# A static scheduler's numbers, the order of the DeltaNet weights and projections issued in passes

## The chip, the cores and the metric

The kernel runs on one core of one Trainium2 chip. The metric is the device time of one execution in microseconds (us), the median of the runs shown. TensorE is the matrix engine (PE in the profile), VectorE is DVE, ScalarE is ACT, GpSimd is POOL, and SyncE (SP) issues most of the transfers.

## What is computed

One sequence of 512 tokens with 1024 channels goes through three layers:

- a layer with dilated band attention and attention to a memory of 256 tokens, then a gated feed-forward network of width 2816;
- a layer whose mixer is a gated DeltaNet with six heads of width 128, in both directions, with the same kind of memory attention, then another feed-forward network;
- a last mixer with gated linear attention, a state-space part and sparse attention, whose sum is projected and added.

The DeltaNet is what matters here, cut to its core:

```python
qkv, z, gate_in, q_mem = split(h @ w_in)
q, k, v = silu(conv5(qkv))                  # q and k also normalized per head
a   = I + strict_lower((k*beta) k^T * decay)   # per head, direction and chunk of 64
sol = triangular_solve(a, [v*beta, k*beta*exp(g)])
for chunk in chunks:                        # the state is carried from chunk to chunk
    v_new = u - w @ state
    out   = (q*exp(g)) @ state + intra @ v_new
    state = state*exp(g_last) + (k*exp(g_last-g))^T @ v_new
o = rmsnorm(o_fwd + o_bwd) * out_norm * silu(z)
```

## The kernel before, in words

All matrices are float32. A projection keeps the precision by splitting each operand into a high and a low part: `wh` is the weight rounded by ScalarE (L243), `wl` is the rest, subtracted by VectorE (L262), and likewise `Xh` and `Xl` for the activations. `mm3` (L268) then issues three matmuls in a row into one bank of PSUM, low weight by high activation (L271), high by low (L272) and high by high (L273). A projection of one weight of 1024 by 128 is eight such blocks of 512 columns. A weight comes as one transfer of 512 KB (L207), through three raw buffers and four split ones.

**The order of the work** is made by `Flow` (L56). Every piece of work is a Python generator that yields requests: an engine and a planned duration, a buffer or bank from a set (`get`, `two`), or an event (`wait`). `Flow.run` keeps a planned free time for each engine. It takes the request that could start first, and among those of the same engine within `DELTA` of it the one with the lowest `late` number; the generator then writes its instructions. So the order of the instructions on each engine is fixed when the program is written, and the chip runs each engine's list in order, waiting where an operand is not there. `HOP` (L63) is the planned time between two engines, and L96 adds 0.07 us where an operation of an engine other than TensorE follows one of its own. `act`, `dve` and `pool` (L151 to L160) are planned durations by elements.

**DeltaNet** (L1168) begins with `projector` (L1775), the generator that projects the weights in the order that `deltanet_weights` (L1158) gives, with `late` 20, so that it fills TensorE where nothing else is ready. The first four weights are done in two halves of tokens. Each result holds one of two banks (`mm`) until it is taken. For each head:

- `key` convolves the projection (four vector operations, L1322), normalizes it and makes the transposed key `kTh`, the scaled copies `ktd` and the products of keys `kk`. Two heads may hold `kTh` and `ktd`; they are given back when a head's chains end.
- `decays` makes for each direction the decay `AT` and the strict lower part `Ln`. It takes a `px` bank for each direction in turn, of three.
- `query` makes `qTh` and the product `kq`, and holds a `px` bank until the decays of both directions are there. `value` and `gate` make `vtok` and `zt` (two heads).
- `inverse` (L1483) inverts the 64-row triangles in six levels and one merging step. A level is 16 small products and four transposes (L1508, L1512), two copies by ScalarE (L1519), 16 products (L1533) and two predicated copies by VectorE (L1537). Each half takes two of three `lv` banks. Two threads run it, one for the even heads and one for the odd ones (`inv=2`). Its result goes to `Uf`, of which there is one.
- `chain` (L1569), one for each direction, carries the state through four chunks (L1580, L1583, L1588, L1591, L1595) and holds a `px` bank all the time. `gate_out` normalizes, transposes and multiplies by the gate (L1645).

`memory` is the attention to the memory (L841), and `splits` prepares the output projection (L1691, L1693). The last mixer uses `projector` too, for 15 single weights and some pieces of two.

Of the kernel before, what the change touches and what calls it, by code (L numbers as in the profile page):

```python
# [35 lines left out]
S = 512  # L36
D = 1024
KT = D // P
# [13 lines left out]

DELTA = 0.1


class Flow:  # L56
# [5 lines left out]

    HOP = 0.2  # L63

# [28 lines left out]
    def start(self, eng, toks):  # L93
        s = self.free[eng]
        for at, e in toks:
            s = max(s, at + (self.HOP if e != eng else 0.0 if e == "PE" else 0.07))  # L96
        return s

    def run(self):
        while self.threads:  # L100
# [39 lines left out]
            s, t = min(ops, key=lambda x: x[0])  # L140
            s, t = min((x for x in ops if x[1]["req"][0] == t["req"][0] and x[0] <= s + DELTA), key=lambda x: x[1]["late"])
            eng, cost = t["req"][:2]
            self.free[eng] = s + cost
            t["tok"] = (s + cost, eng)
# [18 lines left out]
class K:  # L163
# [132 lines left out]
    def inputs(self, F, W, eX, eM, eF, pro):  # L296
# [93 lines left out]
        def memory():  # L390
            yield "late", 0.5
            for l in range(2):
                yield "wait", *eN[l]
                for c in range(2):
                    ev = W["mk"][l][c]
                    yield "wait", ev
                    yield "get", "mm"
                    p = self.psum("mm")
                    w = ev["W"]
                    for k in range(KT):  # L400
                        t = yield "PE", 0.33
                        self.mm3(p[:, :256], (w.h[:, k, :], w.l[:, k, :]), (M[l].h[:, k, :], M[l].l[:, k, :]),
                                 k == 0, k == KT - 1)
                    F.put("wsl", t)
                    F.add(evac(self.memK[l][:, c, :], p), 0.5, t)
                yield "wait", *W["mv"][l]
                for u in range(2):
                    yield "get", "mm"
                    p = self.psum("mm")
                    ts = slice(u * P, (u + 1) * P)  # L410
                    for k in range(KT):
                        w, kk = W["mv"][l][k // 4]["W"], k % 4
                        t = yield "PE", 0.33
                        self.mm3(p[:, :256], (M[l].h[:, k, ts], M[l].l[:, k, ts]), (w.h[:, kk, :], w.l[:, kk, :]),
                                 k == 0, k == KT - 1)
                    F.add(evac(self.memV[l][:, u, :], p, l == 1 and u == 1), 0.5, t)
                for _ in range(2):
                    F.put("wsl", t)
# [118 lines left out]
    def attention(self, F, W, eX, eM, eB, at, e2):  # L537
# [41 lines left out]
        def group(g):  # L579
# [37 lines left out]
            for i, t0 in enumerate((0, 64, 192, 320, 384)):  # L617
                yield "get", "mm"
                p = self.psum("mm")
                for k in range(KT):  # L620
                    w, kk = W2[k // 4]["W"], k % 4
                    t = yield "PE", 0.33
                    self.mm3(p[:, :256], (X.h[:, k, t0:t0 + P], X.l[:, k, t0:t0 + P]), (w.h[:, kk, :], w.l[:, kk, :]),
                             k == 0, k == KT - 1)
                F.add(copy_v(g, i, p[:, :256], r["t"][2][:, i, :], "mm"), g - 0.5, t)
# [394 lines left out]
    def out_ffn(self, F, i, W, gnext, groups, kev, before):  # L1020
# [57 lines left out]
        for part, (f0, f1) in enumerate(self.PARTS):  # L1078
# [22 lines left out]
            while f < nf:  # L1101
                fs = (f, f + 1) if part == 0 and f == 0 else (f,)
                banks = {}
                for hv in ((0, 256), (256, 512)) if len(fs) == 2 else ((0, 512),):
# [3 lines left out]
                    for f_ in fs:  # L1108
                        for z in range(2):
# [6 lines left out]
                            for k in range(KT):  # L1116
                                tk = yield "PE", 0.65 * (t1 - t0) / 512
                                self.mm3(p[:, t0:t1], (ev["W"].h[:, k, :], ev["W"].l[:, k, :]),
                                         (X.h[:, k, t0:t1], X.l[:, k, t0:t1]), k == 0, k == KT - 1)
# [38 lines left out]
    def deltanet_weights(self):  # L1158
# [4 lines left out]
        r["m"] = [self.weight(w, 0, KT, 3096 + c * P, P) for c in range(2)]  # L1163
        N = 3
        heads = [[r[n][h] for n in ("kqvz" if h < N else "kqv")] for h in range(6)]
        return r, [r["g"]] + sum(heads[:3], []) + r["m"] + sum(heads[3:], []) + r["z"][N:]

# [589 lines left out]
    def proj(self, F, ev, eX, m=P):  # L1757
# [7 lines left out]
        for t0, t1 in rngs:  # L1765
            yield "wait", *eX[t0 // P:t1 // P]
            for k in range(KT):
                t = yield "PE", 0.65 * (t1 - t0) / S
                self.mm3(p[:m, t0:t1], (W.h[:, k, :], W.l[:, k, :]), (X.h[:, k, t0:t1], X.l[:, k, t0:t1]),
                         k == 0, k == KT - 1)  # L1770
# [4 lines left out]
    def projector(self, F, items, eX, eP, late=20, haste=0):  # L1775
# [5 lines left out]

        X = self.X
        yield "late", late

        def part(it, t0, t1):
            W, m = it["W"], it["args"][4]
            yield "wait", *eX[t0 // P:t1 // P]
            for k in range(KT):
                t = yield "PE", 0.65 * (t1 - t0) / S
                self.mm3(it["p"][:m, t0:t1], (W.h[:, k, :], W.l[:, k, :]), (X.h[:, k, t0:t1], X.l[:, k, t0:t1]),  # L1790
                         k == 0, k == KT - 1)
            if t1 == S:
# [13 lines left out]
        for i, it in enumerate(items):  # L1806
# [13 lines left out]
            for u in range(4):  # L1820
# [4 lines left out]
                for k in range(KT):  # L1825
                    W, kk = it[k // 4]["W"], k % 4
                    t = yield "PE", 0.33
                    self.mm3(p[:, :256], (X.h[:, k, sl], X.l[:, k, sl]), (W.h[:, kk, :], W.l[:, kk, :]),
# [394 lines left out]
    def s5(self, F, W, eX, open_, eY, uT):  # L2223
# [140 lines left out]
        def glu():  # L2364
# [14 lines left out]
            for c in range(2):  # L2379
                zs = []  # L2380
                for o in (2, 0):
# [3 lines left out]
                    for k in range(2):  # L2385
                        t = yield "PE", 0.65
                        self.mm3(p, (w.h[:, k, os_], w.l[:, k, os_]), yh[k], k == 0, k == 1)
# [898 lines left out]
```

## Time and profile before

| | us |
|---|---|
| median of 3 runs (1770.24 to 1770.43) | 1770.36 |
| the profiled execution | 1771.96 |
| its span from the first to the last instruction | 1770.2 |
| TensorE busy | 1718.8 |
| VectorE busy | 951.0 |
| ScalarE busy | 797.4 |
| GpSimd busy | 276.0 |

In the profile a busy time is a union: the end of a matmul is modelled, and the next one begins before it, so a row of matmuls is read by the time from start to start. "PEclk" is the granted share of TensorE's clock, 1.00 for 2.4 GHz and 0.50 for 1.2 GHz, as a mean over the stretch. An idle time is put down to the instruction that ended it.

### The profile page before, as it was taken

To read this page: it belongs to the slowest core of one execution; us is meant where nothing else is said; L and a number is where in the kernel's file an instruction comes from. 1 tells how busy PE (TensorE), PEld (TensorE's weight loads), DVE (VectorE), ACT (ScalarE), POOL (GpSimd) and SP (SyncE) were. 2 spreads that over 40 slices of the span, in tenths; PEclk is the share of its full clock that TensorE was granted. 3 is DMA by queue.
4 is the path that set the end of the run, shared out by engine and by line. 5 is a ranking of instruction groups with operands and counts; after the bars stand their busy time and mean duration, and the time that the engine had idled before them with its cause. 6 is when DMAs were issued, how large, how long until landed. Compare 5 with 4: busy or idle time off the path is not lost.

```text
span 1770.2 us, 30809 instructions
## 1 busy us (share of the span) xinstructions
PE 1718.8 (97%) x12391; PEld 1431.1 (81%) x12391; DVE 951.0 (54%) x1895; ACT 797.4 (45%) x1922; POOL 276.0 (16%) x440
## 2 busy tenths in 40 slices
PE   6999999999999999999999899999999999999999
PEld 5988679888888887787877778888888888888787
DVE  6333656323333378756765467464433468467573
ACT  5443635333222247657666455333222353345671
POOL 5200001000000020000000152375540033210000
PEclk8999999999999999999999999999999999999999
DMA  6513133333233333102010165344333253552012
GB/s 194 152 51 96 49 119 96 119 96 95 96 95 96 96 119 84 50 26 61 26 49 26 33 157 141 104 146 134 106 108 102 80 154 112 151 160 70 25 37 84
DMA packets 211983, 167.88 MB, mean 95 GB/s; under 512 B 21996, under 2 KB 183036, under 8 KB 211840
## 3 DMA queue, kind: packets, MB, share of 16 engines
q1 hardware_dynamic: 203808, 154.39, 29.6%
q0 software_dynamic: 4560, 9.42, 2.1%
q10 hardware_dynamic: 3472, 2.10, 0.4%
q8 instruction: 97, 1.59, 0.4%
q14 instruction: 46, 0.38, 0.1%
HBM read 152.23 MB, written 13.65 MB: 94 GB/s over the span
## 4 chain that ended last, share of the span: by engine, by line
PE 89%; DVE 6%; ACT 2%; issue 2%; DMA 1%; POOL 1%; ACTq 0%; SPq 0%; DVEq 0%; POOLq 0%
PE bk L271 23%; PE bk L272 23%; PE bk L273 23%; PE x L1508 1%; PE x L1512 1%; PE y L1533 1%; PE no L2740 1%; PE npT L2723 1%; DVE wl L262 1%; DVE hs L940 1%; PE chain L1588 1%; PE ns L2709 1%; PE hT L947 1%; PE ns L2707 1%; PE o L1608 1%
## 5 line engine op out<-in xcount | busy, mean ns | idle before, releaser
L262 DVE TENSOR_TENSOR wl<-raw,wh 128x512 fp32r<-128x512 f32 x450 | 314.7, 740 | 386.7 <-ACT wh L243 386.3
L243 ACT ACTIVATE wh<-raw 128x512 fp32r<-128x512 f32 x474 | 273.0, 622 | 532.9 <-PE bk L273 296.6
L271 PE MATMUL bk<-Xh,wl 128*128 128x512 f32 (+2 forms) x1312 | 494.6, 377 | 0.2 <-ACT Xh L949 0.2
L272 PE MATMUL bk<-Xl,wh 128*128 128x512 f32 (+2 forms) x1312 | 477.9, 364 | 0.5 <-DVE Xl L954 0.3
L273 PE MATMUL bk<-Xh,wh 128*128 128x512 f32 (+2 forms) x1312 | 478.0, 364 | 0.0
L271 PEld LDWEIGHTS bk<-Xh,wl 128*128 128x128 f32 (+1 forms) x1312 | 247.0, 188 | 40.1 <-issue 4.1
L273 PEld LDWEIGHTS bk<-Xh,wh 128*128 128x128 f32 (+1 forms) x1312 | 246.7, 188 | 39.8
L272 PEld LDWEIGHTS bk<-Xl,wh 128*128 128x128 f32 (+1 forms) x1312 | 247.3, 188 | 34.6 <-DVE Xl L954 0.9
L271 PE MATMUL bk<-wh,Xl 128*128 128x512 f32 (+1 forms) x424 | 152.6, 360 | 7.9 <-DVE Xl L794 3.7
L272 PE MATMUL bk<-wl,Xh 128*128 128x512 f32 (+1 forms) x424 | 145.4, 343 | 0.4 <-DVE wl L262 0.4
L273 PE MATMUL bk<-wh,Xh 128*128 128x512 f32 (+1 forms) x424 | 145.5, 343 | 0.0
L271 PE MATMUL bk<-wh,Al 128*128 128x512 f32 x352 | 139.7, 397 | 0.0
L272 PE MATMUL bk<-wl,Ah 128*128 128x512 f32 x352 | 139.5, 396 | 0.0
L273 PE MATMUL bk<-wh,Ah 128*128 128x512 f32 x352 | 138.6, 394 | 0.0
L919 POOL TENSOR_TENSOR nc<-ncm,nhalf 128x1 f32<-128x1 f32 x16 | 11.6, 726 | 666.8 <-DVE ncm L917 664.4
L271 PEld LDWEIGHTS bk<-wh,Xl 128*128 128x128 f32 x424 | 84.9, 200 | 19.2 <-DVE Xl L794 3.1
L1091 DVE TENSOR_TENSOR sg<-sg,bk 128x512 f32<-128x512 f32 x44 | 30.2, 688 | 124.4 <-PE bk L273 119.9
L272 PEld LDWEIGHTS bk<-wl,Xh 128*128 128x128 f32 x424 | 85.0, 201 | 7.7 <-DVE wl L262 1.1
L273 PEld LDWEIGHTS bk<-wh,Xh 128*128 128x128 f32 x424 | 84.6, 200 | 8.0
L271 PEld LDWEIGHTS bk<-wh,Al 128*128 128x128 f32 x352 | 66.0, 188 | 16.1
L273 PEld LDWEIGHTS bk<-wh,Ah 128*128 128x128 f32 x352 | 66.0, 188 | 16.1
L272 PEld LDWEIGHTS bk<-wl,Ah 128*128 128x128 f32 x352 | 66.1, 188 | 15.3
(577 smaller groups left out, 2590.9 us busy)
## 6 DMA issues: line engine op xcount, KB each, us to landing
raw<-in_ffn_w_gate_up_dram SPq DMA_DIRECT2D x88, 512.0 KB, 3.8
raw<-in_ffn_w_down_dram SPq DMA_DIRECT2D x44, 512.0 KB, 3.4
raw<-in_dn_w_in_dram SPq DMA_DIRECT2D x27, 512.0 KB, 3.8
raw<-in_att_w_in_dram SPq DMA_DIRECT2D x20, 512.0 KB, 3.9
raw<-in_w_in_dram SPq DMA_DIRECT2D x20, 512.0 KB, 3.7
raw<-in_mem_w_kv_dram SPq DMA_DIRECT2D x8, 512.0 KB, 3.5
raw<-in_att_w_out_dram SPq DMA_DIRECT2D x8, 512.0 KB, 3.3
xd<-x SPq DMA_DIRECT2D x8, 512.0 KB, 2.6
```

The lines of the kernel that those rows point to most:

```text
L243: nc.scalar.activation(wh[:, sl], ev["raw"][:, sl], AF.Copy)
L262: eng.tensor_tensor(wl[:, sl], raw[:, sl], wh[:, sl].bitcast(F32), op=OP.subtract)
L271: mm(out, A[1], B[0], start=first, stop=False, **kw)
L272: mm(out, A[0], B[1], start=False, stop=False, **kw)
L273: mm(out, A[0], B[0], start=False, stop=last, **kw)
L940: nc.vector.scalar_tensor_tensor(hh[:, hv[i]], x[:, t, hv[i]], r2, r["gain"][:, hv[i]], op0=OP.mult, op1=OP.mult)
L947: nc.tensor.transpose(p[:, k * P:(k + 1) * P], hh[:, i * 512 + k * P:i * 512 + (k + 1) * P], self.ident)
L1091: nc.vector.tensor_tensor(sg, sg, pu, op=OP.mult)
L1508: nc.tensor.matmul(dn8(b[i])[at], lhsT, rhs, start=True, stop=True)
L1512: nc.tensor.transpose(b[d][:, o:o + P], U[:, d, 2 * n:2 * n + 2, :].rearrange("p c q -> p (c q)"), self.ident)
L1533: nc.tensor.matmul(dn8(ys[par])[HB[f], d, n, :], T[d][HB[par], n, f, :], xs[f][HB[par], d, n, :], start=True, stop=True)
L1588: nc.tensor.matmul(b[:, P:2 * P], Uf[:, d, c, :], rh, start=True, stop=True)
```

## The change

It sets other numbers in the scheduler: `DELTA` 0.05 instead of 0.1; between engines 0.04 us instead of 0.2, but 0.2 from TensorE and 0.12 to it; none between operations of one engine, while each operation of VectorE is planned 0.08 us and each of ScalarE 0.07 us longer. A block of three matmuls is planned 0.682 us instead of 0.65 (0.36 instead of 0.33 at 256 columns). In the DeltaNet weights the keys of heads 1 to 3 go ahead of the gates z0 to z2 and of the memory's two weights. In `projector` the three matmuls of a block of a single weight are three requests instead of one, so other work of TensorE can come between them. No instruction is added or removed. The diff, without four more places that change 0.33 to 0.36 or 0.65 to 0.682:

```diff
-DELTA = 0.1
+DELTA = 0.05
...
-    HOP = 0.2
+    HOP = 0.04
+    FROM_PE, TO_PE = 0.2, 0.12
+    STEP = {"DVE": 0.08, "ACT": 0.07}
...
-            s = max(s, at + (self.HOP if e != eng else 0.0 if e == "PE" else 0.07))
+            s = max(s, at + (self.FROM_PE if e == "PE" else self.TO_PE if eng == "PE" else self.HOP) * (e != eng))
...
             eng, cost = t["req"][:2]
+            cost += self.STEP.get(eng, 0.0)
             self.free[eng] = s + cost
...
-                        t = yield "PE", 0.33
+                        t = yield "PE", 0.36
...
-                                tk = yield "PE", 0.65 * (t1 - t0) / 512
+                                tk = yield "PE", 0.682 * (t1 - t0) / 512
...
-        N = 3
-        heads = [[r[n][h] for n in ("kqvz" if h < N else "kqv")] for h in range(6)]
-        return r, [r["g"]] + sum(heads[:3], []) + r["m"] + sum(heads[3:], []) + r["z"][N:]
+
+        k, q, v, z = (r[n] for n in "kqvz")
+        order = [r["g"], k[0], q[0], v[0]]
+        for h in (1, 2, 3):
+            order += [k[h], z[h - 1]] + (r["m"] if h == 3 else []) + [q[h], v[h]]
+        return r, order + [k[4], q[4], v[4], k[5], q[5], v[5], z[3], z[4], z[5]]
...
             for k in range(KT):
-                t = yield "PE", 0.65 * (t1 - t0) / S
-                self.mm3(it["p"][:m, t0:t1], (W.h[:, k, :], W.l[:, k, :]), (X.h[:, k, t0:t1], X.l[:, k, t0:t1]),
-                         k == 0, k == KT - 1)
+                for i, (w, x) in enumerate(((W.l, X.h), (W.h, X.l), (W.h, X.h))):
+                    t = yield "PE", 0.2275 * (t1 - t0) / S
+                    nc.tensor.matmul(it["p"][:m, t0:t1], w[:, k, :], x[:, k, t0:t1], start=k == i == 0,
+                                     stop=k == KT - 1 and i == 2)
```

## Rows read from the trace of the kernel before

**Rows 1.** The page: busy us, share, instructions; TensorE's clock in 40 slices

```profile
PE 1718.8 (97%) x12391; PEld 1431.1 (81%) x12391; DVE 951.0 (54%) x1895; ACT 797.4 (45%) x1922; POOL 276.0 (16%) x440
...
PEclk8999999999999999999999999999999999999999
```

**Rows 2.** Stretches: length, busy us (count) of each engine, PEclk, DMA share, GB/s

```profile
350.00:400.00 50.00, 50.00 (x218) 40.64 (x218) 12.84 (x20) 16.43 (x29) 0.00 (x0) 1.00 0.33 95
898.00:928.00 30.00, 26.86 (x211) 23.00 (x210) 21.59 (x45) 17.31 (x50) 1.01 (x1) 0.92 0.16 54
```

**Rows 3.** Stretches of line L1537 alone: length, DVE busy (count), PEclk, DMA share, GB/s

```profile
700.00:780.00 80.00, 9.50 (x24) 1.00 0.16 41
780.00:813.00 33.00, 0.00 (x0) 0.95 0.18 49
813.00:898.00 85.00, 9.51 (x24) 1.00 0.14 39
898.00:928.00 30.00, 0.00 (x0) 0.92 0.16 54
928.00:991.00 63.00, 9.51 (x24) 0.96 0.09 27
```

**Rows 4.** TensorE's waits, 663 to 1022 us: us in total, times, longest

```profile
PE pk L1333 <- DVE kraw L1303: 3.6, 1, 3.6
PE chain L1588 <- DVE Uf L1558: 2.6, 3, 1.9
PE bk L271 <- DVE Xl L1693: 2.2, 1, 2.2
PE x L1508 <- DVE Ln L1424: 2.2, 1, 2.2
PE poT L1333 <- ACT otok L1642: 1.6, 1, 1.6
PE x L1508 <- DVE U L1537: 1.1, 2, 0.6
PE chain L1588 <- ACT Uf L1546: 0.7, 1, 0.7
...
PE y L1553 <- ACT xT L1519: 0.6, 1, 0.6
```

**Rows 5.** TensorE's instructions in order of time, 917.85 to 918.6: start, us

```profile
917.87 0.38 PE L1588 MATMUL chain<-rhs,Uf 128*128 128x128 f32 x2
918.00 0.47 PE L271 MATMUL bk<-Xh,wl 128*128 128x512 f32 x1
918.32 0.39 PE L272 MATMUL bk<-Xl,wh 128*128 128x512 f32 x1
918.55 0.40 PE L273 MATMUL bk<-Xh,wh 128*128 128x512 f32 x1
```

**Rows 6.** TensorE's groups by line, 663 to 1022 us: count, busy us, mean ns

```profile
L271 PE MATMUL bk<-Xh,wl 128*128 128x512 f32 (+1 forms) x214 | 91.0, 425 | 0.0
L273 PE MATMUL bk<-Xh,wh 128*128 128x512 f32 (+1 forms) x215 | 81.5, 379 | 0.0
```

**Rows 7.** VectorE: a group in 663 to 1022 us; two splits in order of time

```profile
L262 DVE TENSOR_TENSOR wl<-raw,wh 128x512 fp32r<-128x512 f32 x56 | 36.1, 687 | 24.5 <-ACT wh L243 24.4
...
703.26 1.28 DVE L262 TENSOR_TENSOR wl<-raw,wh 128x512 fp32r<-128x512 f32 x2
```

**Rows 8.** DMA issues: count, KB each, us from issue to landing

```profile
raw<-in_dn_w_in_dram SPq DMA_DIRECT2D x27, 512.0 KB, 3.8
```

**Rows 9.** TensorE's waits at the attention's end, 200 to 240 us

```profile
PE bk L271 <- DVE Xl L794: 3.7, 2, 2.8
PE as L656 <- ACT kT L575: 1.3, 1, 1.3
PE mo L896 <- DVE mpT L886: 1.2, 2, 1.0
```

More of the change, by code (lines that the diff above doesn't have):

```diff
@@ L412, in memory @@
                         w, kk = W["mv"][l][k // 4]["W"], k % 4
-                        t = yield "PE", 0.33
+                        t = yield "PE", 0.36
                         self.mm3(p[:, :256], (M[l].h[:, k, ts], M[l].l[:, k, ts]), (w.h[:, kk, :], w.l[:, kk, :]),
@@ L621, in group @@
                     w, kk = W2[k // 4]["W"], k % 4
-                    t = yield "PE", 0.33
+                    t = yield "PE", 0.36
                     self.mm3(p[:, :256], (X.h[:, k, t0:t0 + P], X.l[:, k, t0:t0 + P]), (w.h[:, kk, :], w.l[:, kk, :]),
@@ L1767, in proj @@
             for k in range(KT):
-                t = yield "PE", 0.65 * (t1 - t0) / S
+                t = yield "PE", 0.682 * (t1 - t0) / S
                 self.mm3(p[:m, t0:t1], (W.h[:, k, :], W.l[:, k, :]), (X.h[:, k, t0:t1], X.l[:, k, t0:t1]),
@@ L1775, in projector @@
     def projector(self, F, items, eX, eP, late=20, haste=0):
-        X = self.X
+        X, nc = self.X, self.nc
         yield "late", late
@@ L1788, in part @@
             for k in range(KT):
-                t = yield "PE", 0.65 * (t1 - t0) / S
-                self.mm3(it["p"][:m, t0:t1], (W.h[:, k, :], W.l[:, k, :]), (X.h[:, k, t0:t1], X.l[:, k, t0:t1]),
-                         k == 0, k == KT - 1)
+                for i, (w, x) in enumerate(((W.l, X.h), (W.h, X.l), (W.h, X.h))):
+                    t = yield "PE", 0.2275 * (t1 - t0) / S
+                    nc.tensor.matmul(it["p"][:m, t0:t1], w[:, k, :], x[:, k, t0:t1], start=k == i == 0,
+                                     stop=k == KT - 1 and i == 2)
             if t1 == S:
@@ L1826, in projector @@
                     W, kk = it[k // 4]["W"], k % 4
-                    t = yield "PE", 0.33
+                    t = yield "PE", 0.36
                     self.mm3(p[:, :256], (X.h[:, k, sl], X.l[:, k, sl]), (W.h[:, kk, :], W.l[:, kk, :]),
@@ L2385, in glu @@
                     for k in range(2):
-                        t = yield "PE", 0.65
+                        t = yield "PE", 0.682
                         self.mm3(p, (w.h[:, k, os_], w.l[:, k, os_]), yh[k], k == 0, k == 1)
```

## The prediction

> **What bounds the kernel now.** I read the page first. TensorE is busy for 1718.8 of 1770.2 us, 97%, and its clock is nearly always full [rows 1]. On this reading there are 51 us to win in the whole kernel. A share says nothing of a stage, so the second view is the busy time by stretches. In a feed-forward stretch 218 matmuls fill 50 us, 0.229 us each, with no idle time [rows 2]: 512 columns pass back to back and no order of issue changes that. The same view shows 26.86 us busy out of 30 in the DeltaNet stretch from 898 to 928 us, with 211 much smaller instructions. So the stage to look at is DeltaNet, 663 to 1022 us.
>
> The third view counts one line, the predicated copy L1537, by stretches cut at its first and last copies [rows 3]. Each head's inverse makes 12 of them, so 24 are two heads. Heads 0 and 1 take 80 us, heads 2 and 3 take 85, heads 4 and 5 take 63. Between the pairs lie 33 and 30 us without a single copy. The last pair is the one in which both inverses advance together. The column for TensorE's clock stands at 1.00 in the first two pairs and at 0.95, 0.92 and 0.96 in the two gaps and the last pair: part of each was spent at 1.2 instead of 2.4 GHz, behind moments when TensorE had too little to do.
>
> The fourth view is the list of TensorE's waits in the stage [rows 4]. They are few: 3.6 us at its start for head 0's key, some 4 us at its end (the gate's transposes, the split of the last output), and in between 2.6 + 0.7 us for the block-diagonal Uf, 2.2 us for Ln, 1.1 us for U and 0.6 us for xT.
>
> These views contradict each other only in appearance. Counted by dependent steps, the stage wastes a lot: had the first two pairs run like the third, 17 + 22 = 39 us would be gone, and the gaps besides. But the low-priority projections fill most of that time. TensorE's own work has to be done in any order, so the most that a better order gives is TensorE's idle time plus its slow clock.
>
> **The change part by part.**
>
> *Order of the DeltaNet weights.* The keys k1 and k2 go one projection earlier, k3 three earlier (before z2 and the two memory weights); the gates z0 to z2 go later. The same 27 weights are fetched by the same queue, 512 KB each, landing in 3.8 us [rows 8]; one is needed per eight blocks of 3 x 0.229 = 0.69 us [rows 2], so the fetch stays covered, and I cost it at nothing. If that cover went, it would cost a landing, 3.8 us, once. Nothing else moves on SP's queue, and GpSimd's queue holds the same instructions. The first four weights are the same ones, so the 3.6 us wait for head 0's key stays. One projection is 8 x 0.69 = 5.5 us of TensorE, so head 1's decays can be ready some 5 us sooner, and the second inverse joins the first sooner. z2, which has to hold its bank until head 0's gate tile is free, no longer stands ahead of k3.
>
> *Passes.* Each block of three matmuls becomes three separate requests. A small product that becomes ready now waits on average half a pass instead of half a block, (0.69 - 0.23) / 2 = 0.23 us less. An inverse goes through TensorE 14 times and a chain of one direction ten times, so a head's dependent path is 24 x 0.23, some 6 us, shorter. That shortens waits; it does not add TensorE time to give.
>
> *What the two give.* The waits between the ends, 2.6 + 0.7 + 2.2 + 1.1 + 0.6 = 7.2 us [rows 4], and the slow clock, (1 - 0.95) x 33 + (1 - 0.92) x 30 + (1 - 0.96) x 63 = 1.65 + 2.4 + 2.5 = 6.6 us [rows 3]: 13.8 us together. The lower bound is nothing: the waits could only change places. I take the whole 13.8, since each of these waits is for a product of a single inverse or of decays that came late, and an earlier key and a quicker turn for small products act on both.
>
> *What the passes cost.* After a small product the first matmul of a block takes longer to be followed: from L271 at 918.00 to L272 at 918.32 are 0.32 us, from there to L273 0.23 us [rows 5]. Returning to a projection costs 0.09 us. How often that happens shows in the means: L271 lasts 425 ns and L273 379 ns, 46 ns apart [rows 6], where a returning one is 0.47 against 0.39, 80 ns apart [rows 5]; so 46 / 80 = 57% of 214 blocks, 123, come behind something else. If arrivals are spread evenly, a pass, a third as long, is followed by something else with 1 - 0.43^(1/3) = 25% chance: 642 x 0.25 = 157, 34 more returns, 3.1 us. In the last mixer 15 single weights go through the same function, 120 blocks; the same ratio gives 19 more, 1.7 us. Sum 4.8 us. The bounds are nothing (no more returns than now) and all passes as often interrupted as blocks are now: 642 x 0.57 - 123 = 243, and 137 more in the last mixer, 380 x 0.09 = 34 us. I take 4.8, since small products arrive in time, not by pass.
>
> The Trainium skill speaks to this price (TensorE: Matmul & The Clock Gate, "Step-by-step: what each phase is for"): the queue pulls a weight load ahead of matmuls in flight, so that the next weights load while the current matmul runs. By that alone returning would cost nothing and the sum would lose its 4.8 us. The 0.32 us step in the trace speaks against it here.
>
> *Durations and times between engines.* These change nothing that an instruction does, only the order in which the program writes them. A vector split of 512 elements was planned at 0.61 us and is now at 0.69; the trace has 687 ns [rows 7]. But two of them back to back take 1.28 us [rows 7], so the second starts 0.60 us after the first: the old figure was right for a row of independent operations, the new one for a dependent one. The time between engines falls from 0.20 to 0.04 us except around TensorE, and the margin in which priority beats readiness from 0.10 to 0.05 us. For a vector operation between two TensorE ones both plans agree: 0.2 + 0.61 + 0.2 = 1.01 against 0.2 + 0.69 + 0.12 = 1.01. So I expect small moves with no sign, nothing net. Bound: the waits at the end of the attention, 3.7 + 1.3 + 1.2 = 6.2 us [rows 9], could go, or double.
>
> **Sum.** -13.8 + 4.8 = -9.0 us on the profiled execution's own 1771.96 us: 1763.0. That execution is 1.6 us above the median of the runs shown (1770.36), so the forecast is **1761 us**, 0.5% faster. A difference under 0.2%, 3.5 us, cannot be told from none.
>
> **Rivals.**
>
> *More gain.* The better plan also removes the attention's 6.2 us [rows 9] and the end of DeltaNet, 2.2 + 1.6 us [rows 4]. -9.0 - 6.2 - 3.8 = -19.0: 1751 us. For it: those waits are of the same kind. Against: they stand at the end of a stage, where no other work is left for TensorE. Chance 0.13.
>
> *Free returns.* The weights of a returning pass load unseen, and a pass costs nothing more than a block: -13.8 us, 1757 us. Against it is the 0.32 us step [rows 5]. It is the skill's rule named above. Chance 0.07.
>
> *No change.* The gaps are not made by the order of the weights. At most two heads hold keys, a head's two chains hold two of three banks, and the query's product holds the third while it waits for the second direction's decay, which needs that bank too. That knot is untouched, and both gaps lie where a head's chains run. Then the 7.2 us stay and only the clock's part pays for the passes: -6.6 + 4.8 = -1.8, 1769 us. Chance 0.16.
>
> *Slower.* One mechanism: the projections are cut up. Every return costs 0.09 us, so from 13.8 / 0.09 = 153 more returns on, the gain is gone; at all 380 the kernel is 20 us slower. Halfway, 266 returns, 24 us, +10: 1781 us. For it: 57% of block ends are already followed by something else. Against: nothing in the change makes more small products. Chance 0.22.
>
> **How the numbers follow.** The forecast has 0.42. Faster by over 0.2%: 0.42 + 0.13 + 0.07 = 0.62. Within 0.2%: 0.16. Slower: 0.22. The range starts below the larger gain with free returns (1751 - 5 = 1746) at 1745 and ends at 1780, near the middle of the slower case, which leaves about 0.06 below and 0.11 above. Within the likeliest case alone I would say 1755 to 1766.
>
> **What would show it.** In the changed profile the copies L1537 should stand closer together: under 75 us for the first pair, and a shorter gap before the second. The stretch from 663 us to the first output projection should fall from 359 to about 350 us, with the waits for Uf, Ln and U under 3 us and the clock over 0.97. The first pass's mean should come nearer to the other two, since all three are now interrupted, and the sum of the three per block should rise by less than 0.03 us. The feed-forward stretches should keep 218 matmuls per 50 us. I am wrong if the gaps between the pairs stay over 25 us, if TensorE is as busy as now while the stage is longer (passes too dear), or if the difference arises before 640 or after 1420 us.

## The result and the profile after

The changed kernel takes 1780.59 us (median of 4 runs, 1776.71 to 1782.67) against 1770.39 (4 runs, 1770.24 to 1772.10): the ratio is 1.0053, interval 1.0034 to 1.0072. By this ratio it is slower by about 9 us, where 9 us less had been forecast. The profiled execution after took 1779.85 us with a span of 1778.1, 7.9 more than before.

The page of the changed kernel, its busy times and the clock in 40 slices:

```profile
PE 1720.9 (97%) x12391; PEld 1431.9 (81%) x12391; DVE 948.2 (53%) x1895; ACT 792.7 (45%) x1918; POOL 275.4 (15%) x440
...
PEclk8999999999999999999999899999999999999999
```

Against [rows 1] TensorE does the same 12391 matmuls in 2.1 us more, and idles 57.2 us where it idled 51.4. Its mean granted clock is 0.985 where it was 0.990. Work was not added; some of it came later. To find where, I cut the kernel at a line that every stage has: the low half of the norm's output, eight pieces, the last of which starts when a stage has all that it needs. The columns are the duration's minimum, median and maximum in ns, then the first and the last start in us. Before:

```profile
L954 DVE TENSOR_TENSOR Xl<-hT,Xh x8: 680/684/692, 267.3 to 291.5; 128x512 fp32r<-128x512 f32 x8
L954 DVE TENSOR_TENSOR Xl<-hT,Xh x8: 676/686/692, 636.9 to 662.4; 128x512 fp32r<-128x512 f32 x8
L954 DVE TENSOR_TENSOR Xl<-hT,Xh x8: 679/684/692, 1040.3 to 1064.4; 128x512 fp32r<-128x512 f32 x8
L954 DVE TENSOR_TENSOR Xl<-hT,Xh x8: 679/686/692, 1415.9 to 1442.0; 128x512 fp32r<-128x512 f32 x8
```

After:

```profile
L957 DVE TENSOR_TENSOR Xl<-hT,Xh x8: 679/683/693, 280.0 to 302.1; 128x512 fp32r<-128x512 f32 x8
L957 DVE TENSOR_TENSOR Xl<-hT,Xh x8: 679/684/692, 649.4 to 675.0; 128x512 fp32r<-128x512 f32 x8
L957 DVE TENSOR_TENSOR Xl<-hT,Xh x8: 679/682/692, 1047.6 to 1069.3; 128x512 fp32r<-128x512 f32 x8
L957 DVE TENSOR_TENSOR Xl<-hT,Xh x8: 680/688/693, 1421.8 to 1449.1; 128x512 fp32r<-128x512 f32 x8
```

The differences of the last starts give five stages. All stage times below are read so, and one column more is the time at which the last matmul of the memory's keys and values ends ("memory done").

| us | front (attention) | 1st FFN | DeltaNet | 2nd FFN | last mixer | span | memory done |
|---|---|---|---|---|---|---|---|
| before | 291.5 | 370.9 | 402.0 | 377.6 | 328.2 | 1770.2 | 49.2 |
| after | 302.1 | 372.9 | 394.3 | 379.8 | 329.0 | 1778.1 | 58.7 |
| difference | +10.6 | +2.0 | -7.7 | +2.2 | +0.8 | +7.9 | +9.5 |

The stage that the argument was about did become shorter. What was lost lies ahead of it, in a stage that neither the order of the DeltaNet weights nor the passes touch. How far such a number can be trusted: six kernels with identical code in the front gave 290.3 to 291.5 us, and two with identical code in DeltaNet 392.7 and 391.2. Differences of up to 1.5 us in one stage are not read.

**DeltaNet after.** The predicated copies, now L1543, by stretches cut at their first and last ones (length, VectorE busy and count, clock, DMA share, GB/s), as in [rows 3]:

```profile
721.00:785.00 64.00, 9.51 (x24) 1.00 0.17 43
785.00:805.00 20.00, 0.00 (x0) 1.00 0.21 54
805.00:896.00 91.00, 9.54 (x24) 1.00 0.14 37
896.00:927.00 31.00, 0.00 (x0) 1.00 0.16 52
927.00:990.00 63.00, 9.52 (x24) 0.99 0.14 44
```

The first pair takes 64 us instead of 80, the first gap 20 instead of 33. The second pair is longer, 91 instead of 85, and the second gap stands at 31, where it was 30. TensorE's waits in the stage, 676 to 1026 us (total, times, longest), to be held against [rows 4]:

```profile
PE pk L1339 <- DVE kraw L1309: 3.0, 1, 3.0
PE y L1539 <- ACT xT L1525: 2.8, 4, 2.0
PE bk L274 <- DVE Xl L1699: 2.2, 1, 2.2
PE pq L1339 <- DVE qTh L1309: 1.8, 1, 1.8
PE poT L1339 <- ACT otok L1648: 0.8, 1, 0.8
```

The waits for Uf and Ln are gone from the list. Two others have grown or are new: 2.8 us for xT, 0.6 before, and 1.8 us for head 0's query.

The five stretches above leave out the two ends of the stage. The stage from norm to norm, in the columns of [rows 2] (TensorE, its weight loads, VectorE, ScalarE, GpSimd, each with its count; clock; DMA share; GB/s), before and after, and then the two ends in the changed kernel:

```profile
662.40:1064.40 402.00, 383.53 (x4439) 317.13 (x4440) 262.79 (x554) 249.85 (x689) 46.57 (x71) 0.97 0.22 57
```

```profile
675.00:1069.30 394.30, 379.82 (x4431) 311.55 (x4430) 262.46 (x556) 249.71 (x690) 47.97 (x71) 0.97 0.21 57
676.00:721.00 45.00, 39.73 (x292) 34.05 (x292) 35.70 (x75) 29.88 (x78) 1.12 (x1) 0.92 0.26 71
990.00:1026.00 36.00, 33.74 (x195) 28.03 (x195) 15.59 (x37) 15.10 (x45) 10.14 (x16) 0.88 0.18 54
```

The clock of the whole stage did not change, 0.97 and 0.97. The slow stretches left the middle and came to the ends: before, 663 to 700 us had 0.95 and 991 to 1022 us 0.94. Of the 7.7 us by which the stage got shorter, 4.0 are idle time of TensorE (18.5 us before, 14.5 after) and 3.7 are busy time.

The projections' three passes have means of 405, 398 and 398 ns in the changed kernel. In [rows 6] the first pass of a block stood 46 ns above the others; now all three are nearly alike, and their sum is 19 ns larger.

**The start.** Busy time of the engines in the first 50 us (TensorE, its weight loads, VectorE, ScalarE, GpSimd, each with its count; clock; DMA share; GB/s). Before:

```profile
0.00:50.00 50.00, 35.66 (x201) 30.68 (x202) 32.24 (x45) 28.40 (x53) 28.02 (x36) 0.90 0.64 193
```

After:

```profile
0.00:50.00 50.00, 30.62 (x140) 24.22 (x140) 26.08 (x43) 25.17 (x45) 20.77 (x32) 0.86 0.59 176
```

Every engine does less in the same time, GpSimd 7 us less, TensorE 61 matmuls less, and the memory is done 9.5 us later. What holds them is seen first on GpSimd's timeline (start, duration, instruction, in brackets the idle time before it and what ended it). Before, from 20 us on:

```profile
21.33 0.94 POOL L340 TENSOR_TENSOR irs<-iss,nhalf 128x1 f32<-128x1 f32 x1 [10.57 <-DVE iss L338]
22.26 5.24 POOL L262 TENSOR_TENSOR wl<-raw,wh 128x512 fp32r<-128x512 f32 x3
27.46 0.54 POOL L340 TENSOR_TENSOR irs<-iss,nhalf 128x1 f32<-128x1 f32 x1
27.98 3.48 POOL L262 TENSOR_TENSOR wl<-raw,wh 128x512 fp32r<-128x512 f32 x2
```

After:

```profile
20.74 0.94 POOL L343 TENSOR_TENSOR irs<-iss,nhalf 128x1 f32<-128x1 f32 x1 [9.95 <-DVE iss L341]
23.79 0.92 POOL L343 TENSOR_TENSOR irs<-iss,nhalf 128x1 f32<-128x1 f32 x1 [2.11 <-DVE iss L341]
27.88 0.54 POOL L343 TENSOR_TENSOR irs<-iss,nhalf 128x1 f32<-128x1 f32 x1 [3.17 <-DVE iss L341]
33.32 0.54 POOL L343 TENSOR_TENSOR irs<-iss,nhalf 128x1 f32<-128x1 f32 x1 [4.91 <-DVE iss L341]
35.93 0.65 POOL L462 DMA_DIRECT2D bias_scr<-brow  x1 [2.07 <-DVE brow L459]
...
37.15 3.78 POOL L265 TENSOR_TENSOR wl<-raw,wh 128x512 fp32r<-128x512 f32 x3
```

Before, GpSimd splits weights between the norm powers, from 22.26 us on. After, its list puts all four powers (each waits for a tile of tokens that comes late) and the write of the bias ahead of the first split, and that split waits until 37.15 us. GpSimd stands idle most of that time with work at hand, because an engine runs its list in order. A raw buffer is free only when its weight is split, so the stall goes on to the transfers. GpSimd splits six of the memory's eight weights, and VectorE the first two. SP's waits in the first 60 us, before:

```profile
SPq L207 <- POOL wl L262: 23.5, 6, 6.5
SPq L207 <- DVE wl L262: 20.1, 5, 6.7
```

After, with one wait of 15.2 us:

```profile
SPq L210 <- DVE wl L265: 24.6, 3, 15.2
SPq L210 <- POOL wl L265: 17.7, 6, 5.8
```

This longest wait is ended by a split of VectorE, not of GpSimd: the last one for the memory's second weight. Before, on VectorE's timeline:

```profile
21.17 0.68 DVE L262 TENSOR_TENSOR wl<-raw,wh 128x512 fp32r<-128x512 f32 x1
```

After, and the transfer of the memory's fifth weight, which starts when it is done:

```profile
35.57 0.67 DVE L265 TENSOR_TENSOR wl<-raw,wh 128x512 fp32r<-128x512 f32 x1
36.30 0.38 SPq L210 DMA_DIRECT2D raw<-in_mem_w_kv_dram  x1
```

VectorE's list had put this split behind the scaling of the last tile of tokens, which waited for its power, and behind the bias rows. Before, the fifth weight left at 21.92 us. So two lists are late at once: the fifth weight waits for VectorE, and the sixth, at 39.70 us, for GpSimd.

### The profile page after: what moved, and what is told of

Its sections match the earlier page's. It is cut to its first block, busy times and chain, and to the rows that moved or that the text cites. A ratio compares the mean times of both kernels' runs of the same rounds, so it can differ in the third digit from the quotient of the medians.

```text
span 1778.1 us, 30792 instructions
## 1 busy us (share of the span) xinstructions
PE 1720.9 (97%) x12391; PEld 1431.9 (81%) x12391; DVE 948.2 (53%) x1895; ACT 792.7 (45%) x1918; POOL 275.4 (15%) x440
## 4 chain that ended last, share of the span: by engine, by line
PE 90%; DVE 5%; ACT 2%; issue 1%; DMA 1%; POOL 1%; ACTq 0%; DVEq 0%; POOLq 0%
PE bk L274 19%; PE bk L275 19%; PE bk L276 19%; PE bk L1797 12%; PE x L1518 1%; PE x L1514 1%; PE y L1539 1%; PE no L2747 1%; PE npT L2730 1%; DVE wl L265 1%; DVE hs L943 1%; PE chain L1594 1%; PE ns L2716 1%; PE hT L950 1%; PE ns L2714 1%
## 5 line engine op out<-in xcount | busy, mean ns | idle before, releaser
L274 PE MATMUL bk<-Xh,wl 128*128 128x512 f32 (+1 forms) x912 | 338.2, 371 | 0.8 <-DVE wl L265 0.8
L276 PE MATMUL bk<-Xh,wh 128*128 128x512 f32 (+1 forms) x912 | 334.7, 367 | 0.0
L275 PE MATMUL bk<-Xl,wh 128*128 128x512 f32 (+1 forms) x912 | 334.6, 367 | 0.0
L274 PEld LDWEIGHTS bk<-Xh,wl 128*128 128x128 f32 x912 | 172.0, 189 | 30.5 <-issue 1.8
L276 PEld LDWEIGHTS bk<-Xh,wh 128*128 128x128 f32 x912 | 171.9, 188 | 28.4
L275 PEld LDWEIGHTS bk<-Xl,wh 128*128 128x128 f32 x912 | 172.0, 189 | 27.1 <-issue 0.2
L1797 PE MATMUL bk<-Xh,wl 128*128 128x512 f32 (+2 forms) x400 | 151.2, 378 | 0.0
L1797 PE MATMUL bk<-Xh,wh 128*128 128x512 f32 (+2 forms) x400 | 150.1, 375 | 0.0
L1797 PE MATMUL bk<-Xl,wh 128*128 128x512 f32 (+2 forms) x400 | 149.4, 374 | 0.0
L922 POOL TENSOR_TENSOR nc<-ncm,nhalf 128x1 f32<-128x1 f32 x16 | 10.7, 667 | 685.6 <-DVE ncm L920 683.3
```

Of the source, the lines that this page charges most:

```text
L274: mm(out, A[1], B[0], start=first, stop=False, **kw)
L275: mm(out, A[0], B[1], start=False, stop=False, **kw)
L276: mm(out, A[0], B[0], start=False, stop=last, **kw)
L1797: nc.tensor.matmul(it["p"][:m, t0:t1], w[:, k, :], x[:, k, t0:t1], start=k == i == 0, stop=k == KT - 1 and i == 2)
```

## The experiments

### The two edits of DeltaNet, alone and together

The order of the weights alone:

```diff
-        N = 3
-        heads = [[r[n][h] for n in ("kqvz" if h < N else "kqv")] for h in range(6)]
...
+        order = [r["g"], k[0], q[0], v[0]]
+        for h in (1, 2, 3):
+            order += [k[h], z[h - 1]] + (r["m"] if h == 3 else []) + [q[h], v[h]]
```

> Only the order of the DeltaNet weights is changed; scheduler's numbers and blocks as before. Theory A (the changed kernel's loss arises in front of DeltaNet and comes from the scheduler's numbers; order and passes together shorten DeltaNet): the splits of the last norm before DeltaNet end at 663 us as before, DeltaNet to the next norm's end takes about 398 instead of 402 us, total 1766 us. Theory B (DeltaNet's gain too comes from the numbers, the order does nothing): 402 us again, total 1770 us.

Measured: 1767.14 us, ratio 0.9991 (0.998 to 1.0002), not to be told from none; DeltaNet 398.0 us, 4.0 less than before, front 290.3.

The passes alone, in DeltaNet and the last mixer:

```diff
-                t = yield "PE", 0.65 * (t1 - t0) / S
-                self.mm3(it["p"][:m, t0:t1], ...
+                for i, (w, x) in enumerate(((W.l, X.h), (W.h, X.l), (W.h, X.h))):
+                    t = yield "PE", 0.2275 * (t1 - t0) / S
+                    nc.tensor.matmul(it["p"][:m, t0:t1], ...
```

> Only the projections' three passes are separate requests. Theory A: front as before (663 us), DeltaNet about 398 instead of 402 us, the last mixer 1 to 2 us longer than its 327.5, total 1767 us. Theory B: DeltaNet 402 us, total 1770 to 1772 us. A third, that returning to a projection costs what the slower rival said: DeltaNet 410 us or more, total 1780 us.

Measured: 1764.15 us, 0.9962 (0.995 to 0.9975). DeltaNet 391.2 us, 10.8 less; the last mixer 332.2 us, 4.0 more.

Both:

```diff
+        order = [r["g"], k[0], q[0], v[0]]
...
+                    t = yield "PE", 0.2275 * (t1 - t0) / S
```

> Order of the DeltaNet weights and separate passes, with the scheduler's old numbers. Theory A: front as before (663 us), DeltaNet 394 us as in the changed kernel, last mixer about 328.5, total 1763 us. Theory B: DeltaNet 402 us, total 1770 to 1772 us.

Measured: 1769.31 us, 0.9999 (0.9989 to 1.0009). DeltaNet 396.3: the two together bring 5.7 us, less than the passes alone. They do not add.

The passes in DeltaNet only; the last mixer keeps its blocks:

```diff
             for k in range(KT):
+                if haste:
+                    t = yield "PE", 0.65 * (t1 - t0) / S
+                    self.mm3(it["p"][:m, t0:t1], ...
+                    continue
+                for i, (w, x) in enumerate(((W.l, X.h), (W.h, X.l), (W.h, X.h))):
```

> The kernel before with separate passes in DeltaNet's projections alone, blocks in the last mixer. Theory A (passes help where a chain of small products is in the way, and in the last mixer they only change which work is left for its end): DeltaNet 391 us, last mixer 327.5, total 1759 us. Theory B (the last mixer's 4 us in the run with passes everywhere come from the order that DeltaNet leaves): last mixer 331, total 1763 us.

Measured: 1760.09 us, 0.9939 (0.9924 to 0.9954). DeltaNet 392.7, last mixer 327.9. The 4.0 us of the second experiment do come from the passes in the last mixer and go when blocks stand there again. TensorE's waits from 662 to 1013 us in this kernel:

```profile
PE x L1508 <- DVE Ln L1424: 3.5, 2, 3.2
PE pk L1333 <- DVE kraw L1303: 2.3, 1, 2.3
```

The wait for Ln is still there, 3.5 us against 2.2 in [rows 4]. The passes shorten the stage by 9.3 us without taking away the wait that was to go.

### The scheduler's numbers

All of them, without order and passes:

```diff
-DELTA = 0.1
+DELTA = 0.05
...
-    HOP = 0.2
+    HOP = 0.04
+    FROM_PE, TO_PE = 0.2, 0.12
+    STEP = {"DVE": 0.08, "ACT": 0.07}
...
-                t = yield "PE", 0.65 * (t1 - t0) / S
+                t = yield "PE", 0.682 * (t1 - t0) / S
```

> Only the scheduler's durations, times between engines and margin are changed. Theory A: the first feed-forward's norm ends at 303 us as in the changed kernel (292 before), the norm before DeltaNet at 676, DeltaNet 402 us, total 1782 to 1788 us. Theory B: front as in the changed kernel too, but DeltaNet 394 us, total 1779 to 1781 us.

Measured: 1796.14 us, 1.0151 (1.0128 to 1.0175). Front 300.8 (+9.3), memory done at 58.2, DeltaNet 401.9, last mixer 337.4 (+9.2). The loss in the front is the numbers' alone. So is one in the last mixer that the changed kernel does not show: with order and passes beside the numbers it takes 329.0.

The longer operations alone:

```diff
+    STEP = {"DVE": 0.08, "ACT": 0.07}
...
+            cost += self.STEP.get(eng, 0.0)
```

> The kernel before with one number changed: each VectorE operation is planned 0.08 us and each ScalarE operation 0.07 us longer. Theory A (longer planned vector work makes the plan put the weights' splits on GpSimd behind the norms' small operations, so the weight transfers starve in the first 50 us): the first feed-forward's norm ends at 298 to 303 us (292 before), total 1776 to 1790 us. Theory B (the smaller margin for priority does it): front as before, 292 us.

Measured: 1798.30 us, 1.0155 (1.0139 to 1.0172). Front 293.1, first FFN 373.8, DeltaNet 412.5 (+10.5), second FFN 380.9, last mixer 338.9 (+10.7). Memory done at 49.1: the start is not its doing.

The longer operations with the new times between engines:

```diff
-    HOP = 0.2
+    HOP = 0.04
+    FROM_PE, TO_PE = 0.2, 0.12
+    STEP = {"DVE": 0.08, "ACT": 0.07}
```

> The kernel before with the added vector durations and the new times between engines together. With the added durations alone DeltaNet took 412.5 us and the last mixer 338 (402 and 327.5 before). Theory A (longer operations and shorter times between engines make up for each other, as the prediction's 1.01 = 1.01 said): DeltaNet 400 to 404 us, last mixer 328 to 333, front 292 to 296. Rival (longer planned vector work harms by itself): DeltaNet 410 us or more, total 1795 us.

Measured: 1780.84 us, 1.006 (1.0045 to 1.0075). DeltaNet 402.2 and last mixer 328.4, as before the change: the two do cancel there. The feed-forward networks keep 375.4 and 379.9, 4.5 and 2.3 more.

The narrower margin alone:

```diff
-DELTA = 0.1
+DELTA = 0.05
```

> The kernel before with the margin for priority alone at 0.05 instead of 0.1 us. Theory A (the margin makes the front's loss, because at its half the attention's products no longer go ahead of the projections that could start a little sooner): last projection of the attention near 204 us, its tail from there to the last broadcast of the mixture's weights over 34 us (30 before), norm of the first feed-forward at 297 us or more. Rival (the margin only matters together with the planned durations): front 291 to 293 us, total within 4 us of 1770.

Measured: 1767.04 us, 0.9978 (0.9967 to 0.9988). DeltaNet 396.6 (-5.4), last mixer 326.0 (-2.2), front 293.1, memory done at 46.9. By itself the margin is a gain and does not delay the start.

The longer matmuls alone:

```diff
-                t = yield "PE", 0.65 * (t1 - t0) / S
+                t = yield "PE", 0.682 * (t1 - t0) / S
```

> The kernel before with TensorE's planned durations alone (0.682 and 0.36 instead of 0.65 and 0.33). Theory A (a minor part): front 292 to 294 us, total 1768 to 1774 us. Rival (the share of the front that vector numbers leave unexplained is here): front 296 us or more.

Measured: 1785.87 us, 1.0093 (1.0074 to 1.0112). Front 299.3 (+7.8) with the memory done at 50.4, last mixer 339.5 (+11.3), DeltaNet 399.5. A plan that is 5% nearer to the trace costs about 16 us.

The changed kernel with the old margin:

```diff
-DELTA = 0.05
+DELTA = 0.1
```

> The changed kernel with the old margin, 0.1 us. Theory A: front 293 to 296 us instead of 303, total 1768 to 1772 us. Rival (durations and times between engines make it, not the margin): front 300 us or more, total 1777 us or more.

Measured: 1791.06 us, 1.0123 (1.0106 to 1.014). Front 291.5, as before the change, memory done at 49.0; but DeltaNet 403.8 and last mixer 339.0. In company with the other numbers the narrower margin costs 10.6 us in the front and brings 9.5 and 10.0 us later. That it was harmless alone shows that a number has no price of its own here.

The changed kernel with the old times, durations of VectorE and ScalarE, and margin until DeltaNet begins:

```diff
+    HOP = FROM_PE = TO_PE = 0.2
+    OWN, DELTA, STEP = 0.07, 0.1, {}
...
+                F.numbers()
                 eK, eP, close = self.deltanet(F, W1, order1, eX, res)
```

> The changed kernel, but the scheduler keeps the old times between engines, no added durations and the old margin until DeltaNet begins; TensorE's planned durations are the new ones throughout. Theory A (the loss is in front and is made by these numbers): norm of the first feed-forward at 292 us, DeltaNet 394, second feed-forward 379, last mixer 328, total 1765 us. Theory B (the loss follows from the passes or TensorE's durations): norm at 300 us or more, total 1775 us or more.

Measured: 1769.03 us, 0.9992 (0.9979 to 1.0005). Front 293.4, memory done at 48.5, DeltaNet 392.9. The loss of the front is gone and the gain of DeltaNet has stayed: the two are separate.

### What delays the start

The order of the splits on VectorE and GpSimd is one candidate, SP's order the other: after the change two late tiles of tokens stand on SP's queue ahead of the memory's weights. First, the two tiles held back on SP's queue:

```diff
                 yield "late", -5 if i < NF else 0.05
+                if i in (4, 5):
+                    yield "wait", W["mv"][i - 4][5 - i]["got"]
```

> The changed kernel with one edit: the third and fourth tile of x are loaded only behind the fourth and the seventh weight, as the kernel before orders them. Theory A: the wait of the weight queue for a vector split in the first 60 us falls from 15 us, TensorE is busy 33 us or more of the first 50 (30.6 in the changed kernel), norm of the first feed-forward at 293 to 297 us, total 1772 us. Rival (the tail of the attention, where the clock fell to 0.90, makes the loss by itself): norm at 301 to 303 us, total 1780 us.

Measured: 1778.15 us, 1.0037 (1.0024 to 1.005). Memory done at 55.0, front 301.2. With 167 matmuls in the first 50 us TensorE gets 27 of the 61 lost ones back, the last projection of the attention ends 4.1 us earlier, and the front is 0.9 us shorter. But this is not SP's old order, nor a test of it alone: the last tile leaves behind the eighth weight, at 42.37 us, where before it left at 29.68, ahead of it; and the splits move too, GpSimd's first one to 24.72 us. So it does not clear SP's order; it shows that this edit brings little.

Next, the tokens first in the kernel before, without any change of numbers:

```diff
-                yield "late", -5 if i < NF else 0.05
+                yield "late", -5
```

> The kernel before with one number of one generator changed, so that all tiles of x are asked for first. That puts all four powers of the norms of x and the write of the bias rows ahead of every weight split in GpSimd's list, as in the changed kernel; nothing of the scheduler's numbers changes. Theory A' (GpSimd's order starves the weights): the memory's last matmul at 55 to 59 us instead of 49, last projection of the attention at 208 to 210 us instead of 203. Rival (the late weights come from the planned durations, not from this order): 49 to 51 us and 203 to 204 us.

Measured: 1779.79 us, 1.0055 (1.004 to 1.007). Front 300.2 (+8.7), memory done at 59.4, all later stages as before. So an order at the start alone, with the old numbers, makes a loss of this size. But it does not part the lists: VectorE's splits and GpSimd's both come later, and SP's queue, too, waits for the tokens' buffers. SP's waits of this kernel, first 60 us:

```profile
SPq L207 <- DVE wl L262: 23.0, 3, 18.7
...
SPq L318 <- DVE hs L343: 8.1, 2, 5.9
```

A cleaner one: the changed kernel, with the old margin for the first 60 planned us only. SP's list stays as in the changed kernel; GpSimd's gets its splits between the powers again. The lists of VectorE and ScalarE change with it.

```diff
-... and x[0] <= s + DELTA), ...
+... and x[0] <= s + (2 * DELTA if s < 60 else DELTA)), ...
```

> The changed kernel with the old margin for the first 60 planned us alone. The transfers stand in the same order as in the changed kernel, but five weight splits stand ahead of the write of the bias rows on GpSimd. Theory A': the memory's last matmul at 49 us (58.7 in the changed kernel), last projection at 203 us, norm of the first feed-forward at 292 to 297 us, total 1768 to 1773 us. Rival (the attention's tail is long by itself and takes up what the start gives): last projection at 203 us but the norm at 300 us or more, total 1778 us.

Measured: 1770.68 us, 1.0003 (0.9993 to 1.0013), 9.9 less than the changed kernel. Memory done at 49.5, front 295.3. Its first 50 us:

```profile
0.00:50.00 50.00, 35.20 (x206) 29.13 (x207) 30.05 (x45) 29.44 (x54) 29.59 (x36) 1.00 0.67 198
```

GpSimd's first split and VectorE's last one for the second weight, on their timelines:

```profile
23.59 5.84 POOL L265 TENSOR_TENSOR wl<-raw,wh 128x512 fp32r<-128x512 f32 x3
27.01 1.29 DVE L265 TENSOR_TENSOR wl<-raw,wh 128x512 fp32r<-128x512 f32 x1
```

GpSimd's split is back at 23.59 us and VectorE's stands at 27.01 instead of 35.57, TensorE has 206 matmuls in 50 us, and 6.8 of the front's 10.6 us are gone. With SP's list unchanged this is the order of the other lists at the start. Both lists of splits moved, so which of them holds the memory up is not separated.

**The rest of the front**, 295.3 - 291.5 = 3.8 us, lies at its end. TensorE's waits from 203 to 262 us in the changed kernel, which answer to [rows 9]:

```profile
PE fbc L765 <- DVE amx L757: 3.0, 1, 3.0
PE as L659 <- ACT kT L578: 2.2, 1, 2.2
PE bk L274 <- DVE Xl L797: 1.7, 1, 1.7
PE ms_t L883 <- DVE mp L874: 1.6, 2, 0.8
PE mo L899 <- DVE ams L745: 0.9, 1, 0.9
```

With two smaller ones they make 10.2 us; before it was 6.7 in that stretch. With the start mended they still make 11.0, and with the longer matmuls alone 10.2. The projections, which fill TensorE, are over by then (at 203.3 us before, 202.3 with the start mended), and the dependent chain of the attention goes on alone: from there to the last broadcast of the mixture's weights (fbc) it is 37 us in the changed kernel and 38 with the start mended, 30 before. For the longer matmuls alone these waits account for 3.5 of the 7.8 us, a later last projection for 1.7; 2.6 us are left open. The granted clock from 200 to 262 us goes the same way: 0.97 before, 0.92 in the changed kernel and with the start mended, 0.86 with the longer matmuls alone. What part of the time it makes, no run separates.

### A version that beats both

Passes in DeltaNet only, the old numbers, and the narrower margin from the last mixer on:

```diff
                 tst.close()
+                F.DELTA = 0.05
                 st.enter_context(self.second(F, W3, eX, res, out))
...
+                if haste:
```

> The kernel before with separate passes in DeltaNet alone, and the margin 0.05 us from the last mixer on. If stages add up: front to second feed-forward as with the passes in DeltaNet alone, last mixer 325 instead of 327 us, total 1758 us. If a stage's plan depends on the state in which the one before leaves the engines: last mixer 330 us or more, total 1762 us or more.

Measured: 1757.57 us (1756.40 to 1757.88), 0.9928 (0.9914 to 0.9943) of the kernel before, some 12 to 13 us less. Front 290.4 and the feed-forward networks 370.3 and 377.6 stand as before the change, DeltaNet is 391.2, the last mixer 326.2. The margin's own part is the 1.7 us of the last mixer against the version without it (327.9), hardly more than the 1.5 us that are not read; the other 1.5 us between the two lie in DeltaNet, whose code is the same.

## Why the prediction was wrong

**Durations and times between engines: the step that failed.** "Small moves with no sign, nothing net", bounded by 6.2 us, was an argument about the plan's sum for one operation between two of TensorE's: 1.01 against 1.01. That sum holds where it was made: longer operations alone lengthen DeltaNet by 10.5 us, and with the times between engines it is 402.2 again. But a plan does more than add up one chain. It decides at each moment between requests that could start within the margin of each other, and each list is run in that order. The fifteen kernels show what a single number can do to one stage: +11.3 us (last mixer, longer matmuls), +10.5 (DeltaNet, longer operations), -5.4 (DeltaNet, margin). A term of nothing, bounded by 6.2 us, stood for all of them together; alone they make the kernel 1.5% slower, 22.3 us of span (1792.5 against 1770.2). In the changed kernel they cost the front 10.6 us. Taking the bound from the waits at the end of the attention [rows 9] looked at one place of the 1770 us. Those waits did grow, by 3.5 us; the larger part came from the start, of which no row had been read.

**"GpSimd's queue holds the same instructions"** was true and beside the point: it holds them in another order, and so does VectorE's. The order of the lists in the first 60 planned us made 6.8 us of the loss. Here the prediction had named one of these queues and costed it at nothing, without reading what stood on it in the first 40 us. The remark was made of the order of the weights, and so was "Nothing else moves on SP's queue"; for the new numbers neither queue was looked at, and with them the two late tiles go ahead of weights on SP's queue.

**What the two give: right in place and sign, but not by the clock.** For DeltaNet the steps gave -13.8 + 3.1 = -10.7 us; measured are -7.7. The 6.6 us of the slow clock were not won. In four of the five stretches of [rows 3] the clock is 1.00 now and in the last 0.99, but the stage as a whole has 0.97 as before. The slow stretches came to 676 to 721 us (0.92) and 990 to 1026 us (0.88), which the term, taken from 700 to 991 us, did not look at. There they stand beside idle time of TensorE: the wait of 3.0 us for head 0's key, which ends at 697.9 us, that of 2.0 us for xT, which ends at 987.0, and that of 2.2 us for the last output's split, which ends at 1019.4. So here the slow clock went with the waits that changed their place. The waits' term was too large: all of TensorE's waits from 676 to 1026 us are 11.1 us now and were 15.6 ([rows 4] and two of 0.2 and one of 0.6 us), 4.5 gained where 7.2 were taken. Part of them did change places, which the step had named as its lower bound. Against them stand some 3.4 us of returns, so the 3.7 us less of busy time are not explained. Nor do the experiments let the credit stand as it was given: the passes alone bring 10.8 us, the order alone 4.0, both 5.7, the margin alone 5.4. Why they don't add is not settled; no run separates it.

**The knot of the "No change" rival is half there.** The first gap between pairs fell from 33 to 20 us, the second stayed, 31 us where it was 30. The banks as the cause were argued, not tested.

**What the passes cost: right in DeltaNet.** The prediction took 123 returns from the means and added 34. Counted in the trace, a projection's matmul follows something else 109 times before and 149 times after, 40 more. From the start of the first matmul after something else to the next one is 0.315 us in the median, against 0.227 to 0.231 otherwise: 0.084 to 0.088 us each, 0.09 by [rows 5]. The rule of the Trainium skill that was weighed against this row (TensorE: Matmul & The Clock Gate, "Step-by-step: what each phase is for") would have the next weights load unseen. In the return of [rows 5] they do not: the load for L271 runs from 917.98 to 918.17 us, beside the matmul that is recorded from 918.00 on, while the next one's begins 0.23 us ahead of its matmul. In the last mixer 11 more returns came where 19 were forecast, but the price was another one: with passes alone there are only 5 more and the stage is 4.0 us longer, with 2.7 us of waits of TensorE from 1680 to 1715 us, where the last work is left with nothing beside it; before there were 0.3. Over the whole mixer the waits are 5.8 us and were 2.3, which makes 3.5 of the 4.0. The cost of cutting up lies there in the waits and not in the returns.

**The rivals.** "Slower" had the sign and the time, 1781 us, but by returns, and these did not come: that it met the time is luck. The forecast's own list of tests held for DeltaNet: the first pair's copies in 64 us (under 75), a shorter gap before the second, the stretch to the first output projection 676 to 1026 us, 350 long, a clock of 0.98 in it (but it had been 0.97), no waits for Uf or Ln, pass means 7 ns apart and their sum up by 0.019 us. It held in the feed-forward stretch too, from 350 to 400 us of the changed kernel: 218 matmuls at a clock of 1.00.

Two of the tests of failure were met: a gap over 25 us, and a difference that arises before 640 us. The 2 us by which each feed-forward network is longer lie outside this stretch. For the first they are there in every kernel that plans longer operations of VectorE and ScalarE at that time (372.9 to 375.4) and in none without (370.3 to 371.0); for the second it is less clear (379.3 and 379.7 in two kernels without). Which operation is late was not followed.

## What to carry to other kernels

Where a planner writes the lists, a new number is a new program: read each stage against the old one, and first the start, where the buffers are empty and one operation in the wrong place on a quiet engine can hold the transfers of all. Numbers nearer to the trace did not make a better plan here, and their effects don't add; change one at a time, and let it hold only for the stage in which it gains. A part that is right on its own (passes in DeltaNet, -9.3 us) is best sent alone, since its gain can vanish in what comes with it.

## What the runs showed of the hardware that was not expected

VectorE and GpSimd slow each other. Scaling a tile of tokens on VectorE took 2.29 us before, while GpSimd split weights (27.98 to 31.46 us, two in 3.48, as shown above):

```profile
28.04 2.29 DVE L346 SCALAR_TENSOR_TENSOR hs<-xs,irs,rowx 128x1024 f32<-128x1024 f32 x1 [0.54 <-POOL irs L340]
```

In the changed kernel, with GpSimd idle at that moment, it took 1.28 us:

```profile
28.45 1.28 DVE L349 SCALAR_TENSOR_TENSOR hs<-xs,irs,rowx 128x1024 f32<-128x1024 f32 x1 [0.20 <-POOL irs L343]
```

So the later splits of the changed kernel even bought VectorE some time, and the front was longer all the same. The Trainium skill (SBUF — State Buffer, "Who interferes with whom") has the two engines share one pair of ports. By it a VectorE instruction with two inputs in SBUF contends with a GpSimd one that reads SBUF, and whichever comes first blocks the other. The trace nearly agrees: a split alone takes 1.26 us (three in 3.78, above), and two splits and the scaling one after another would be 1.26 + 1.28 + 1.26 = 3.80 us, where 3.48 are seen.

The other surprise is the size of what the order of in-order lists does on engines that are far from full. VectorE is busy 53% of the time and GpSimd 15%. GpSimd was idle for most of 21 to 37 us, and the order of the lists in that time was worth 6.8 us.
